# Gate matrix from float32 one-hots, all first products in split halves, block 1's second products on VectorE

## The chip, the cores and the metric

The kernel is one program on one core of a Trainium2 chip. The metric is the device time of one execution in microseconds (us). The engines are called as in the profile: PE is TensorE (PEld its weight loads), DVE is VectorE, ACT is ScalarE, POOL is GpSimd, SP is SyncE, which here issues only DMAs.

## The reference

Two layers work on 512 tokens of width 1024. Each layer is a token mixer (four heads of differential attention and eight of stick-breaking attention) with a LayerNorm, and then PEER, a retrieval over 128 x 128 experts of one neuron each, with a LayerNorm:

```python
q = (xt @ w_query).reshape(T, PEER_HEADS, 2, HALF_Q)
scores = jnp.einsum('thpc,hpnc->thpn', q, sub_keys)
top_s, top_i = lax.top_k(scores, PEER_TOPK)
# ... the 16 best of the sums of both halves, per head: idx, gate = softmax(best_s)
u = expert_u[ic]                                            # 128 experts for each token
act = jax.nn.gelu(jnp.einsum('cd,ced->ce', xc, u), approximate=False)
v = expert_v[ic]
y = jnp.einsum('ce,ced->cd', gc * act, v)
h = layer_norm(DEEPNORM_ALPHA * h + y, ln2_g[l], ln2_b[l])
```

All arrays are float32. Each of the 512 tokens selects 8 x 16 = 128 of the 16384 experts.

## The kernel before

The tokens are four blocks of 128. PEER is computed in two ways that run side by side.

**Blocks 0 and 1 (`BLK_A`) gather.** `indices` selects the experts of a block (`select`, mostly DVE). `gathers` then fetches one row of `expert_u` for each token at a time: POOL issues an indirect DMA of 128 rows of 4 KB, and one DVE instruction (`dot`, "row<-row,ha" in the profile) multiplies it with the tokens and sums. There are 128 such gathers in a block, with six buffers (`gat`). After the GELU the second products follow. For a block in `TOK` (before: both blocks) `token_products` does them on PE: the rows of `expert_v` of one token at a time ("row<-v,idxT") are multiplied by a column of weights in a sliding window (`win`), four matmuls of 32 columns for two tokens. For a block outside `TOK` the function `add` does them on DVE, one gather of `expert_v` rows ("row<-v,idx") and one multiply-add of 128 x 1024 for each of the 128 selections ("ha<-row,c,ha"). The blocks go one after the other: `done["turn ..."]` starts block 1 when block 0 has its products, and layer 1's block 0 when layer 0's block 1 has them. The last instructions of `gathers` are the residual, LayerNorm and, in layer 1, the store of the output.

**Blocks 2 and 3 (`BLK_B`) are dense.** `gates` makes the matrix of gates of all 16384 experts for a block. For four tokens at a time (`NT`) it makes one-hot vectors of the two halves of the expert's number, multiplies one of them by the gate, and PE multiplies the two; the result goes to DRAM (`gdram`, "gd"). Before, the one-hots are bfloat16, and the gate is three bfloat16 pieces, so that a token costs three matmuls; the pieces are spread over ACT, POOL and DVE by `pick`. `dense` goes over 32 chunks of 512 experts: `first` (products with `expert_u` and GELU), `weigh` (the transposed result times the gates, and its halves), `second` (products with `expert_v`, accumulated in four PSUM banks over all chunks). `second` waits for the gates of both blocks. A chunk's weights are 2 MB for `first` and 2 MB for `second`. Except in the first `AHEAD` = 7 chunks of `first`, they are split into two float32r halves by `split`: ACT makes the upper half, and POOL or DVE (by `pick`) subtracts it ("t<-st,t", four parts for each of `first` and `second`); three float32r matmuls take the place of one float32 matmul. The first seven chunks, which run before the gates are ready, use the raw float32 weights on PE ("native").

**What sets the order.** All these are Python generators. `run_threads` holds a planned time for each engine and lets the thread with the smallest ready time less its `lead` go on; `cost(...)` is what a step takes in that plan. An engine named in `soft` doesn't hold the step back. The scheduler behind it fixes one instruction order for each engine, and `bound` keeps instructions within a distance of the plan. So on the chip each engine takes its instructions in a fixed order, and an instruction that waits holds up those behind it. `rest` runs layer after layer: the mixer of blocks 1, 2 and 3, then `dense`. The mixer of layer 1 takes block 1 first, so it starts when block 1 of layer 0 has its LayerNorm; `early` runs the mixer of block 0 ahead. The helper at line 70 (72 in the changed kernel) records every instruction, so all rows have that line.

## Time and profile before

| | us |
|---|---|
| median of three runs | 3627.01 (3624.92 to 3645.93) |
| profiled execution | 3652.87, span 3651.1 |

| engine | busy us | share of the span |
|---|---|---|
| PE | 3081.1 | 84% |
| PEld | 2236.5 | 61% |
| DVE | 2332.3 | 64% |
| POOL | 1802.7 | 49% |
| ACT | 1169.6 | 32% |

The DMA engines move 1035 MB, 284 GB/s over the span. A share over the whole span mixes stages: in layer 0 the mixer and the gates take up to about 1012 us, the dense products up to 1988, and block 1's gathers lie beside them; layer 1 follows in the same order, with its second products from 2870 to 3636. Idle time of an engine costs only where it is the one the others wait for, so the stages are read one by one. A float32 matmul has two records in the profile, a float32r or bfloat16 matmul one.

### The profile page before, as it was taken

The page shows a single profiled execution, that of the slowest core. Times are in us where ns is not written, and L with a number is a line of the kernel's source. Part 1 is how long each engine was busy: PE and PEld are TensorE (multiplying, and loading weights), DVE is VectorE, ACT ScalarE, POOL GpSimd, SP SyncE. Part 2 cuts the span into 40 slices and gives each one's busy share as a digit, 9 for nine tenths or more (in the row PEclk, how much of TensorE's full clock was granted, in tenths as well). Part 3 has the DMA queues.
Part 4 walks back from the last instruction along what each step waited for, and adds up shares of the span by engine and source line. Part 5 has one row for each costly group of instructions (what it writes and reads, how often), then busy time and mean ns, then how long its engine had stood idle before and what let it go on. Part 6 is the DMA issues. An engine that isn't in the chain of part 4 may idle for free.

```text
span 3651.1 us, 45407 instructions
## 1 busy us (share of the span) xinstructions
PE 3081.1 (84%) x16660; PEld 2236.5 (61%) x16660; DVE 2332.3 (64%) x4974; ACT 1169.6 (32%) x1867; POOL 1802.7 (49%) x1368
## 2 busy tenths in 40 slices
PE   7995597888788868899997597888987699999998
PEld 5774473653566756766665486647535577766665
DVE  2588768375668698633336756576757888864335
ACT  2112652120414223333332016613215344343332
POOL 0266426244446375354537752254555666654443
PEclk9997698898889989999999697988997799999999
DMA  5689576577596877689898984566785999989996
GB/s 222 235 331 336 173 268 216 194 262 277 208 364 256 321 279 293 229 329 352 314 347 300 355 321 163 216 235 244 266 305 186 342 345 337 355 295 335 332 355 247
DMA packets 285215, 1035.19 MB, mean 284 GB/s; under 512 B 25408, under 2 KB 91456, under 8 KB 232768
## 3 DMA queue, kind: packets, MB, share of 16 engines
q0 software_dynamic: 147456, 536.94, 40.4%
q1 hardware_dynamic: 137536, 495.36, 36.2%
q8 instruction: 131, 2.15, 0.2%
q14 instruction: 92, 0.75, 0.1%
HBM read 991.30 MB, written 38.80 MB: 282 GB/s over the span
## 4 chain that ended last, share of the span: by engine, by line
PE 33%; issue 9%; POOL 7%; DVE 5%; DMA 4%; ACT 3%; POOLq 0%; another core or an unknown queue 0%; SPq 0%; DVEq 0%; ACTq 0%
PE ps L70 33%; POOL row L70 4%; POOL t L70 3%; DVE d L70 2%; DMA row<-v,idxT 2%; ACT d L70 1%; DVE t L70 1%; ACT L70 1%; DVE row L70 1%; DMA t<-gd 1%; ACT t L70 1%; DMA st<-ut 0%; DMA gd<-st 0%; DVE idf L70 0%; POOL d L70 0%
## 5 line engine op out<-in xcount | busy, mean ns | idle before, releaser
L70 POOL DMA_INDIRECT row<-v,idxT x512 | 566.6, 1107 | 819.0 <-PE ps L70 672.9
L70 PE MATMUL ps<-t,d 128*128 128x512 f32 (+1 forms) x3232 | 808.4, 404 | 147.1 <-POOL t L70 48.9
L70 POOL DMA_INDIRECT row<-u,idx x512 | 672.1, 1313 | 430.1 <-DVE row L70 239.7
L70 PEld LDWEIGHTS ps<-t,d 128*128 128x128 f32 x3232 | 609.6, 196 | 340.3 <-ACT t L70 69.1
L70 DVE SCALAR_TENSOR_TENSOR row<-row,ha 128x1024 f32<-128x1024 f32 x512 | 673.1, 1330 | 164.8 <-DMA row<-u,idx 142.7
L70 DVE TENSOR_TENSOR t<-st,t 128x1024 fp32r<-128x1024 f32 x344 | 472.2, 1412 | 451.6 <-ACT t L70 391.4
L70 PE MATMUL ps<-t,t 128*128 128x512 f32 (+1 forms) x3040 | 664.9, 382 | 15.6 <-DVE t L70 6.9
L70 PEld LDWEIGHTS ps<-t,t 128*128 128x128 f32 (+1 forms) x3040 | 523.1, 197 | 160.3 <-issue 43.3
L70 PE MATMUL ps<-t,st 128*128 128x128 f32 x4096 | 505.8, 284 | 20.9 <-issue 8.9
L70 PEld LDWEIGHTS ps<-t,st 128*128 128x128 f32 x4096 | 491.3, 199 | 42.2 <-issue 27.7
L70 ACT ACTIVATE t<-st 128x1024 fp32r<-128x1024 f32 x456 | 452.8, 1050 | 113.8 <-PE ps L70 88.1
L70 PE MATMUL ps<-st,t 128*128 128x512 f32 x960 | 452.5, 621 | 8.9 <-DMA st<-ut 6.6
L70 POOL TENSOR_TENSOR t<-st,t 128x1024 fp32r<-128x1024 f32 x112 | 284.5, 2551 | 214.0 <-ACT t L70 167.9
L70 ACT ACTIVATE t<-ps 128x512 f32<-128x512 f32 (+1 forms) x192 | 88.8, 492 | 824.8 <-PE ps L70 798.7
L70 PE MATMUL ps<-row,win 128*32 128x512 f32 x2048 | 288.0, 646 | 74.5 <-DMA row<-v,idxT 73.3
L70 PEld LDWEIGHTS ps<-st,t 128*128 128x128 f32 x960 | 183.3, 200 | 247.4 <-issue 241.7
L70 PE MATMUL ps<-d,d 128*128 128x128 bf16 (+1 forms) x1792 | 252.2, 295 | 74.1 <-POOL d L70 30.1
L70 PEld LDWEIGHTS <-d 128*128 128x128 bf16 x1536 | 174.3, 119 | 116.0 <-issue 72.2
L70 ACT COPY st<-ps 128x256 f32<-128x256 f32 x256 | 137.0, 646 | 254.1 <-PE ps L70 216.4
L70 ACT COPY t<-ps 128x512 f32<-128x512 f32 (+4 forms) x180 | 81.1, 459 | 381.0 <-PE ps L70 340.3
L70 DVE TENSOR_TENSOR d<-iota_b,d 128x512 bf16<-128x512 bf16 x246 | 137.5, 598 | 97.5 <-PE ps L70 97.3
L70 POOL TENSOR_TENSOR d<-d,d 128x512 bf16<-128x512 bf16 x132 | 150.8, 1163 | 79.3 <-issue 42.5
(118 smaller groups left out, 2339.6 us busy)
## 6 DMA issues: line engine op xcount, KB each, us to landing
st<-ut SPq DMA_DIRECT2D x128, 1024.0 KB
st<-vd SPq DMA_DIRECT2D x128, 1024.0 KB
st<-w_in SPq DMA_DIRECT2D x48, 1024.0 KB
st<-w_query SPq DMA_DIRECT2D x48, 1024.0 KB
gd<-st SPq DMA_DIRECT2D x32, 1024.0 KB
t<-gd SPq DMA_DIRECT2D x64, 512.0 KB
st<-w_o SPq DMA_DIRECT2D x24, 1024.0 KB
ln<-ln SPq DMA_DIRECT2D x16, 512.0 KB
```

The lines of the kernel that those rows point to most:

```text
L70: r = f(*args, **kwargs)
```

## The change

The one-hots become float32: for each token one `tensor_scalar` makes the one-hot of one half, and one makes the other half's one-hot times the gate, both on DVE; a token then costs one float32 matmul. The plan gives them to DVE alone. `NATIVE = 0` sends the first seven chunks of `first` through `split` as all others. `TOK = [0]` takes block 1 out of `token_products`: its second products go through `add` on DVE. `pace` holds DVE as `soft` for block 0 only, so that block 1's steps wait for DVE's place in the plan. The thread `gates` is spawned with a lead of 40 in place of 6.

```diff
@@ -46,7 +46,9 @@
 HH = PH // 2
 AHEAD = 7
 
-TOK = [0, 1]
+NATIVE = 0
+
+TOK = [0]
 
 REACH = 8
 
@@ -216,8 +218,8 @@
     iota_c = const.tile([P, NCAND, TOPK], BF16, name="iota_c")
     nc.gpsimd.iota(iota_c, pattern=[[1, NCAND], [0, TOPK]], base=0, channel_multiplier=0,
                    allow_small_or_imprecise_dtypes=True)
-    iota_b = const.tile([P, P, NT], BF16, name="iota_b")
-    nc.gpsimd.iota(iota_b, pattern=[[1, P], [0, NT]], base=0, channel_multiplier=0,
+    iota_b = const.tile([P, P], F32, name="iota_b")
+    nc.gpsimd.iota(iota_b, pattern=[[1, P]], base=0, channel_multiplier=0,
                    allow_small_or_imprecise_dtypes=True)
 
 
@@ -563,7 +565,7 @@
                 if n % 2 == 0:
                     SC.setdefault((l, b), []).append(fold(t4(), 8))
                     if n == 0 and b in BLK_B:
-                        spawn(gates(l, b), 6.0)
+                        spawn(gates(l, b), 40.0)
                 ps = psum()
                 for f in range(4):
                     for c in range(DC):
@@ -740,7 +742,7 @@
         c = sel.tile([P, NSEL], F32, name="c")
 
         def pace(dve):
-            return cost(lat=1.2, soft="DVE", DVE=dve, POOL=1.04, DMA=1.6)
+            return cost(lat=1.2, soft="DVE" if b == BLK_A[0] else "", DVE=dve, POOL=1.04, DMA=1.6)
 
         def row(src, s):
             g = gat.tile([P, D], F32, name="row")
@@ -805,7 +807,7 @@
         for half in range(2):
             yield from select(l, b, half, idf, gate)
         idf, gate = (t.rearrange("p h k -> p (h k)") for t in (idf, gate))
-        yield cost(lat=3.0, DVE=2.0, PE=0.7)
+        yield cost(lat=3.0, DVE=1.2, PE=0.7, ACT=0.4)
         ii = a2(I32)[:, :2 * NSEL].rearrange("p (a k) -> p a k", a=2)
         nc.vector.tensor_copy(ii[:, 1, :], idf)
         nc.vector.tensor_single_scalar(ii[:, 0, :], ii[:, 1, :], 7, op=ALU.arith_shift_right)
@@ -815,55 +817,28 @@
         pt = psum()
         for n, src in enumerate((fi[:, 0, :], fi[:, 1, :], gate)):
             nc.tensor.transpose(pt[:, n * P:(n + 1) * P], src, ident)
-        t0, t1 = a2(), a2()
-        gp, ij = fold(t0[:, :3 * P], 3), fold(t0[:, 3 * P:].bitcast(BF16), 2)
-        ijf, gb = fold(t1[:, :2 * P], 2), fold(t1[:, 2 * P:2 * P + 3 * P // 2].bitcast(BF16), 3)
-        nc.vector.tensor_copy(ij.rearrange("p a t -> p (a t)"), pt[:, 0:2 * P])
-        nc.scalar.copy(ijf.rearrange("p a t -> p (a t)"), pt[:, 0:2 * P])
-
-        nc.vector.tensor_copy(gp[:, 0, :], pt[:, 2 * P:3 * P])
-        for k in range(3):
-            nc.vector.tensor_copy(gb[:, k, :], gp[:, k, :])
-            if k < 2:
-                nc.vector.tensor_sub(gp[:, k + 1, :], gp[:, k, :], gb[:, k, :])
-                nc.vector.tensor_copy(gp[:, k, :], gb[:, k, :])
-        shp = [P, P, NT]
-
-        def hots(tg, t0):
-            t = tg * GT + t0
-            hot = a2h().rearrange("p (a j t) -> p a j t", a=2, t=NT)
-            for n in range(2):
-                if pick(ACT=1.7, DVE=0.34) == "ACT":
-                    for k in range(NT):
-                        nc.scalar.activation(hot[:, n, :, k], iota_b[:, :, k], AF.Abs, scale=-1.0,
-                                             bias=ijf[:, n, t + k:t + k + 1])
-                    nc.scalar.activation(hot[:, n], hot[:, n], AF.Relu, scale=-1.0, bias=1.0)
-                else:
-                    nc.vector.tensor_tensor(hot[:, n], iota_b, ij[:, n, t:t + NT].unsqueeze(1).to_broadcast(shp),
-                                            op=ALU.is_equal)
-            w01 = a2h().rearrange("p (a j t) -> p a j t", a=2, t=NT)
-            w2 = a2h()[:, :P * NT].rearrange("p (j t) -> p j t", t=NT)
-            ws = (w01[:, 0], w01[:, 1], w2)
-            for k, w in enumerate(ws):
-                eng = pick(ACT=1.2, POOL=1.0, DVE=0.34)
-                if eng == "ACT":
-                    for n in range(NT):
-                        nc.scalar.activation(w[:, :, n], hot[:, 0, :, n], AF.Copy, scale=gp[:, k, t + n:t + n + 1])
-                else:
-                    (nc.gpsimd if eng == "POOL" else nc.vector).tensor_tensor(
-                        w, hot[:, 0], gb[:, k, t:t + NT].unsqueeze(1).to_broadcast(shp), op=ALU.mult)
-            return hot, ws
+        ijg = fold(a2()[:, :3 * P], 3)
+        nc.scalar.copy(ijg.rearrange("p a t -> p (a t)"), pt[:, :3 * P])
+
+        def hots(t):
+
+
+            hot, w = (fold(a2(), NT) for _ in range(2))
+            for k in range(NT):
+                nc.vector.tensor_scalar(hot[:, k, :], iota_b, ijg[:, 1, t + k:t + k + 1], None, op0=ALU.is_equal)
+                nc.vector.tensor_scalar(w[:, k, :], iota_b, ijg[:, 0, t + k:t + k + 1],
+                                        ijg[:, 2, t + k:t + k + 1], op0=ALU.is_equal, op1=ALU.mult)
+            return hot, w
 
         stg = {}
 
-        def products(tg, t0, hot, ws):
+        def products(tg, t0, hot, w):
             if t0 == 0:
                 stg[tg] = [fold(st_tile().rearrange("p c f -> p (c f)"), 64) for _ in range(2)]
             ps = psum()
             for n in range(NT):
-                for k, w in enumerate(ws):
-                    nc.tensor.matmul(ps[:, n * P:(n + 1) * P], lhsT=hot[:, 1, :, n], rhs=w[:, :, n],
-                                     start=(k == 0), stop=(k == 2))
+                nc.tensor.matmul(ps[:, n * P:(n + 1) * P], lhsT=hot[:, n, :], rhs=w[:, n, :],
+                                 start=True, stop=True)
             ps = fold(ps, NT)
             for a in range(2):
                 nc.scalar.copy(stg[tg][a][:, :, t0:t0 + NT].rearrange("p i t -> p t i"),
@@ -875,8 +850,8 @@
 
         todo = []
         for t in range(0, P, NT):
-            yield cost(lat=0.7, ACT=0.55, PE=0.8)
-            todo.append((t // GT, t % GT, *hots(t // GT, t % GT)))
+            yield cost(lat=1.6, DVE=1.6, ACT=0.9, PE=1.0)
+            todo.append((t // GT, t % GT, *hots(t)))
             if len(todo) > 1:
                 products(*todo.pop(0))
         products(*todo.pop(0))
@@ -901,7 +876,7 @@
 
         def first(ec):
 
-            native = ec < AHEAD
+            native = ec < NATIVE
             for a in range(2):
                 if native:
                     yield cost(PE=6.9, DMA=2.92)
```

The order of the instructions moves with it. Three places of DVE's order follow; names are tiles of the program with their numbers.

**The end of the program.** Names: "t" with "ps" is the residual of a dense block, which needs the last matmul of `second`; "ha" is block 1's result. Before:

```order
L70 TENSOR_TENSOR t_24433<-st,t_24432 128x1024
L70 TENSOR_TENSOR t_24449<-st,t_24448 128x1024
L70 SCALAR_TENSOR_TENSOR ha<-ha 128x1024
L70 BN_STATS aln_st<-ha 128x6 x2
L70 BN_AGGR aln_mv<-aln_st 128x2
L70 TENSOR_SCALAR aln_ve<-aln_mv 128x1
L70 TENSOR_SCALAR ha<-ha,aln_mv,aln_rs 128x1024
L70 TENSOR_TENSOR ha<-ha,row 128x1024 x2
L70 SCALAR_TENSOR_TENSOR t_24478<-t_24478,ps 128x512 x2
L70 SCALAR_TENSOR_TENSOR t_24482<-t_24482,ps 128x512 x2
```

With the change the dense blocks' residual comes earlier in the order, with five more adds between its instructions, and then:

```order
L72 SCALAR_TENSOR_TENSOR ha<-row,c,ha 128x1024
L72 TENSOR_TENSOR t_23764<-t_23764,ln 128x1024
L72 SCALAR_TENSOR_TENSOR ha<-row,c,ha 128x1024 x65
L72 SCALAR_TENSOR_TENSOR ha<-ha 128x1024
L72 BN_STATS aln_st<-ha 128x6 x2
L72 BN_AGGR aln_mv<-aln_st 128x2
L72 TENSOR_SCALAR aln_ve<-aln_mv 128x1
L72 TENSOR_SCALAR ha<-ha,aln_mv,aln_rs 128x1024
L72 TENSOR_TENSOR ha<-ha,row 128x1024 x2
```

Block 1's result stood before the dense residual; now it stands behind it, with 65 adds of 128 x 1024 ahead of it.

**The end of layer 0's dense products**, with the change; "t_12720" is a dense block's residual in its LayerNorm, and "row<-row,ha" are dots of layer 1's block 0:

```order
L72 SCALAR_TENSOR_TENSOR ha<-row,c,ha 128x1024
L72 TENSOR_TENSOR t_12720<-t_12720,ln 128x1024
L72 SCALAR_TENSOR_TENSOR ha<-row,c,ha 128x1024 x57
L72 SCALAR_TENSOR_TENSOR ha<-ha 128x1024
L72 BN_STATS aln_st<-ha 128x6 x2
L72 BN_AGGR aln_mv<-aln_st 128x2
L72 TENSOR_SCALAR aln_ve<-aln_mv 128x1
L72 SCALAR_TENSOR_TENSOR row,c<-row,ha 128x1024
L72 TENSOR_SCALAR ha<-ha,aln_mv,aln_rs 128x1024
```

Before, the same place reads:

```order
L70 TENSOR_TENSOR ha<-ha,row 128x1024 x2
L70 SCALAR_TENSOR_TENSOR t_13164<-t_13164,ps 128x512 x2
L70 SCALAR_TENSOR_TENSOR row,c<-row,ha 128x1024
L70 BN_STATS ln_st<-t_13164 128x6
L70 SCALAR_TENSOR_TENSOR t_13174<-t_13174,ps 128x512
```

Block 1 had its LayerNorm ("ha<-ha,row") ahead of the dense residual; now 57 adds stand between the two.

**A chunk of layer 1's dense products.** "t<-st,t" is a part of `split`, "row<-row,ha" a dot, "t<-ps,t" and "d<-t,d" are `weigh`. Before:

```order
L70 TENSOR_TENSOR t_21287<-st,t_21286 128x1024
L70 TENSOR_TENSOR t_21303<-st,t_21302 128x1024
L70 TENSOR_TENSOR t_21327<-st,t_21326 128x1024
L70 SCALAR_TENSOR_TENSOR row,c<-row,ha 128x1024
L70 TENSOR_TENSOR t_21343<-st,t_21342 128x1024
L70 SCALAR_TENSOR_TENSOR row,c<-row,ha 128x1024 x2
L70 TENSOR_TENSOR t_20993<-ps,t_21183 128x512 x2
L70 SCALAR_TENSOR_TENSOR row,c<-row,ha 128x1024
L70 TENSOR_TENSOR d_21192<-t_20993,d_21191 128x512
```

With the change:

```order
L72 TENSOR_TENSOR t_20405<-st,t_20404 128x1024
L72 TENSOR_TENSOR t_20421<-st,t_20420 128x1024
L72 SCALAR_TENSOR_TENSOR row,c<-row,ha 128x1024 x2
L72 TENSOR_TENSOR t_20442<-st,t_20441 128x1024
L72 TENSOR_TENSOR t_20458<-st,t_20457 128x1024
L72 TENSOR_TENSOR t_20481<-st,t_20480 128x1024
L72 TENSOR_TENSOR t_20497<-st,t_20496 128x1024
L72 TENSOR_TENSOR t_20184<-ps,t_20377 128x512 x2
L72 TENSOR_TENSOR d_20386<-t_20184,d_20385 128x512
```

Between one `weigh` and the next DVE had six splits and seven dots there (POOL had the other two splits); now it has all eight splits, with seven dots or, later, seven adds.

## Rows read from the trace of the kernel before

**Rows 1.** The page: the span, and each engine's busy time (share, count)

```profile
span 3651.1 us, 45407 instructions
PE 3081.1 (84%) x16660; PEld 2236.5 (61%) x16660; DVE 2332.3 (64%) x4974; ACT 1169.6 (32%) x1867; POOL 1802.7 (49%) x1368
```

**Rows 2.** Busy time by stretch: five engines, granted clock, DMA share, GB/s

```profile
875.00:1012.00 137.00, 101.21 (x580) 61.53 (x579) 83.06 (x171) 43.65 (x78) 64.59 (x55) 0.84 0.68 244
1012.00:1407.00 395.00, 321.17 (x1557) 255.43 (x1557) 314.43 (x601) 113.59 (x166) 228.03 (x143) 0.90 0.81 304
1407.00:1988.00 581.00, 551.85 (x2641) 394.47 (x2641) 281.29 (x278) 204.90 (x252) 275.16 (x188) 0.99 0.84 309
1988.00:2045.00 57.00, 3.67 (x20) 3.12 (x20) 45.05 (x75) 2.25 (x4) 40.29 (x32) 0.54 0.92 330
2700.00:2870.00 170.00, 107.79 (x556) 67.39 (x557) 127.04 (x202) 59.50 (x131) 109.15 (x94) 0.76 0.67 242
2870.00:2952.00 82.00, 76.57 (x330) 61.82 (x330) 73.52 (x79) 31.32 (x37) 57.66 (x33) 0.92 0.92 340
2952.00:3217.00 265.00, 252.86 (x1143) 205.62 (x1142) 221.28 (x264) 109.87 (x132) 162.39 (x94) 1.00 0.92 345
3217.00:3636.00 419.00, 411.00 (x2020) 281.05 (x2018) 185.84 (x177) 145.51 (x180) 193.39 (x145) 0.99 0.87 320
```

**Rows 3.** Timeline of PE in layer 1's dense products: start, duration, count

```profile
2964.16 11.05 PE L70 MATMUL ps<-t,t 128*128 128x512 f32 x48
2975.05 1.04 PE L70 MATMUL ps<-ident,t 128*128 128x128 f32 x8
```

**Rows 4.** Timeline of DVE: the gates' multiply in `weigh`, one row a chunk

```profile
2968.57 1.28 DVE L70 TENSOR_TENSOR t<-ps,t 128x512 f32<-128x512 f32 x2
...
3161.68 1.28 DVE L70 TENSOR_TENSOR t<-ps,t 128x512 f32<-128x512 f32 x2
...
3275.67 1.46 DVE L70 TENSOR_TENSOR t<-ps,t 128x512 f32<-128x512 f32 x2
...
3568.74 1.28 DVE L70 TENSOR_TENSOR t<-ps,t 128x512 f32<-128x512 f32 x2
```

**Rows 5.** Timeline: the instruction nearest to a one-hot, with POOL beside it

```profile
1101.83 5.70 DVE L70 TENSOR_SCALAR dg<-ident,rc 128x128 f32<-128x128 f32 x2
1102.68 4.74 POOL L70 TENSOR_TENSOR t<-st,t 128x1024 fp32r<-128x1024 f32 x2
...
2130.64 0.94 POOL L70 DMA_INDIRECT row<-u,idx  x1 [0.31 <-issue]
...
2130.86 0.47 DVE L70 TENSOR_SCALAR dg<-ident,rc 128x128 f32<-128x128 f32 x2
```

**Rows 6.** Groups by form, 875 to 1012: count | busy us, mean ns | idle before

```profile
L70 PE MATMUL ps<-d,d 128*128 128x128 bf16 x384 | 53.8, 295 | 8.9 <-DVE d L70 8.0 <-POOL d L70 0.7
L70 DVE TENSOR_TENSOR d<-d,d 128x512 bf16<-128x512 bf16 x75 | 40.3, 583 | 0.6 <-PE ps L70 0.6
L70 PE MATMUL ps<-st,t 128*128 128x512 f32 x81 | 39.6, 611 | 0.0
L70 DVE TENSOR_TENSOR d<-iota_b,d 128x512 bf16<-128x512 bf16 x64 | 29.3, 497 | 37.3 <-PE ps L70 37.3
```

**Rows 7.** Groups by form, 2952 to 3217: splits and dots (columns as rows 6)

```profile
L70 DVE TENSOR_TENSOR t<-st,t 128x1024 fp32r<-128x1024 f32 x68 | 104.3, 1549 | 44.6 <-ACT t L70 44.6
L70 DVE SCALAR_TENSOR_TENSOR row<-row,ha 128x1024 f32<-128x1024 f32 x76 | 98.4, 1300 | 0.0
L70 ACT ACTIVATE t<-st 128x1024 fp32r<-128x1024 f32 x88 | 87.0, 1057 | 13.5 <-PE ps L70 13.5
```

**Rows 8.** Busy time of instructions on a gathered row, by stretch (columns as rows 2)

```profile
300.00:400.00 100.00, 0.00 (x0) 0.00 (x0) 69.77 (x116) 74.89 (x59) 0.62 0.91 328
```

**Rows 9.** Groups by form, whole span: all instructions of the kind in rows 5

```profile
L70 DVE TENSOR_SCALAR dg<-ident,rc 128x128 f32<-128x128 f32 x64 | 24.7, 406 | 0.0
```

**Rows 10.** Timeline of POOL: a gather issued while DVE works through its dots

```profile
2003.04 1.98 POOL L70 DMA_INDIRECT row<-u,idx  x1 [0.30 <-issue]
```

## Prediction

> **What bounds it now.** I read the page first: PE is busy for 84% of 3651 us, DVE for 64% [rows 1]. That suggests PE, so I read the stretches next. From 1407 to 1988 and from 2870 to 3636 the dense products run; PE is busy for 93% to 98% there, at a granted clock of 0.92 to 1.00 [rows 2]. The timeline gives the price of a chunk on PE: 48 matmuls of `first` take 11.05 us, those of `second` (same shape) as long, two sets of transposes 1.04 each: 24.2 us [rows 3]. The chunks of 2968 to 3161 come every 24.1 us (193.1 us over eight), so there PE alone sets the pace, while block 1's dots run beside it. From 3276 to 3569 they come every 29.3 us (293.1 over ten) [rows 4]: there block 1's second products are on PE too. DVE is far from full in that second half (185.84 of 419 us), but nearly so in the first (221.28 of 265) [rows 2].
>
> Three other stretches are not PE's. From 875 to 1012 and from 2700 to 2870, the wait for block 3's gates, PE is busy for 74% and 63%, at clocks of 0.84 and 0.76 [rows 2]. From 1012 to 1407 the gathers of block 1 meet the early mixer: DVE 80%, DMA 0.81 [rows 2]. From 1988 to 2045, between the layers, PE does 3.67 us of work [rows 2].
>
> **The change, stretch by stretch.**
>
> *Gates.* In the order, 157 of the 336 split matmuls of `first` and block 3's 128 products of one-hots stand behind that block's selection in layer 0. The nearest row to a one-hot is a DVE tensor_scalar of 128 x 128 float32 with a per-partition scalar: two in 0.47 us, so 0.235 each, even with a gather running [rows 5]. Block 3's 256 cost 60 us of DVE, where the bfloat16 form took 40.3 + 29.3 us in the same stretch, and POOL and ACT had more [rows 6]. On PE a float32 product costs as much as a float32 transpose, 0.26 us (four, two records each, in 1.04 [rows 3]): 33 us for 128, against 53.8 [rows 6]. The 157 split matmuls cost 157 x 0.23 = 36 us, where native ones took 39.6 [rows 6]. So PE needs 69 us, DVE 60 plus some ten splits at 1.4 = 74. I take 87 us in place of 137, a gain of 50, and leave the rest for waits. In layer 1, 97 split matmuls remain at that point: 33 + 22 on PE, 60 and some eight splits on DVE. With most of block 1's early dots gone from there I take 105 in place of 170, a gain of 65. The splits that now come earlier (28 for each layer, 1.06 us of ACT each [rows 7]) lie beside block 0's second products and the projections on PE, with ACT busy for 32% [rows 1]; if that cover fails, they cost 30 us a layer.
>
> *1012 to 1407.* The order has 57 dots where 99 stood, and 51 DVE splits where 32 stood: 42 x 1.3 less 19 x 1.5 [rows 7] frees 26 us of DVE, and 42 gathers of 0.52 MB fewer at 304 GB/s [rows 2] free up to 72 us of DMA. I take 40, between the two.
>
> *1407 to 1988.* Nineteen full chunks, three without `first` and 512 records of block 1's products make 2832 PE records; 2641 are there [rows 2], some being lost. Without block 1 on PE, nineteen chunks at 24.4 and three at 13.2 (11.05 and two transposes) give 503 in place of 581. I take 75, since DVE now has all eight splits: 20.1 us a chunk (221.28 over eleven [rows 2]) plus two splits of at most 1.55 [rows 7] is 23.2, 95% of 24.4. What hides the dots and adds is PE's 24.2 us; without that cover the chunk would cost what DVE needs.
>
> *2870 to 3636.* Five chunks as before, 82; 24 at 24.4 and three at 13.2: 707 in place of 766. I take 56.
>
> *The ends.* Here the change gives back. `add` costs no more than a dot, 1.30 [rows 7]. But 128 dots and 128 adds at seven a chunk need 36 chunks, and the dense products end before. Behind layer 0's dense residual stand four adds and then 57, behind layer 1's five and 65. A row alone costs what its gather does: 59 gathers in 100 us with no dense work beside them, 1.7 us each [rows 8]. In layer 0, 55 rows (six are already in buffers) make 94 us, with 15 for the LayerNorms ahead and 8 for block 1's own. Since the mixer of layer 1 takes block 1 first, PE waits for all of it: 117 in place of 57, a loss of 60. Layer 1's dots start that much later against the dense end, but 49 of them stand in a row ahead of the attention before and after, so nothing more is late. At the end, 64 x 1.7 = 109 and 16 more take the place of the 15 us after 3636: a loss of 110.
>
> *Sum.* -50 - 65 - 40 - 75 - 56 + 60 + 110 = -116: 3535 us on the span of 3651 [rows 1]. The median of the runs stands at 3627, 24 below the profiled span, so I scale: 3535 x 3627 / 3651 = 3512. The rest I price at nothing: the shorter iota at the start, and block 1's index transpose and its small SP transfers (16 fall to 8), which go beside the dense chunks; SP's and POOL's queues keep their other DMAs.
>
> **What I cannot read.** A one-hot (two operations, compare and multiply) may cost more than 0.235: the pair beside two POOL subtractions took 5.70 us [rows 5], but in the order POOL keeps 43 subtractions in place of 112. At 0.41, the mean of all such instructions with their collisions [rows 9], block 3's one-hots cost 45 us more in each layer, +90. A lower price gains nothing, as PE then sets the stretch. A row in the tails costs from 1.25 us (0.94 for the issue and 0.31 ahead of it [rows 5]) to 2.28 (1.98 and 0.30, with DVE busy throughout [rows 10]): -54 to +69 over 119 rows. I take 1.7, since it is measured with DVE and POOL both free to pace each other. A chunk costs from 24.2 (PE's work) to 28: that is DVE's 23.2 over the 0.835 busy share it reached in that stretch [rows 2]. Over 43 chunks that is -9 to +155. I take 24.4, because there PE idled for only 5% with DVE at 84%.
>
> The row beside a gather shows the tensor_scalars going through while POOL issues: the gather runs from 2130.64 to 2131.58, the pair from 2130.86 to 2131.33 [rows 5]. The Trainium skill, "SBUF — State Buffer", section "Who interferes with whom", says otherwise: tensor_scalar can enter a two-port mode, and then whichever of VectorE and GpSimd issues first shuts the other out for the whole instruction. By that rule each one-hot could wait for a gather, or a gather for it. The trace agrees for POOL's subtractions (5.70 us) and not for this gather.
>
> **Rivals.**
> 1. *DVE takes PE's place in the dense products* and the kernel ends slower. For: DVE works at 95% of a chunk by my own sum, its order is fixed, and a dot that waits for its row holds the splits behind it, for which PE waits. Against: at 84% PE lost only 5%, and POOL's slow subtractions leave the path. At 28 us a chunk the span is 3535 + 155 = 3690, which is 3666. It decides from 27.9 us a chunk on (3535 + 3.5 x 43 = 3686, or 3662).
> 2. *The gates give nothing.* The order gives PE and ACT the same chunks to do before the gates, and another wait, for scores or w_query, may set 1012 and 2870. For: PE was already at 74% there. Against: DVE alone spent 70 of 137 us on the one-hots there [rows 6], and that work shrinks on every engine. The span is 3535 + 115 = 3650, so 3626: no change.
> 3. *One-hots and gathers shut each other out.* Block 0's 256 gathers of `expert_v` rows run beside block 2's one-hots; if each held DVE for 0.94 [rows 5], that is 241 us of DVE in stretches where it is not full. I put half on the path: 3535 + 120 = 3655, so 3631. The one gather row speaks against it. This is what the Trainium skill's rule above would do here.
> 4. *The tails are cheaper and the early stretch gains more.* At 1.25 us a row (-54) and the DMA's whole 72 us in 1012 to 1407 (-32) the span is 3449, so 3426.
>
> **How the numbers follow.** My forecast has a chance of 0.56, rival 1 0.12, rival 2 0.14, rival 3 0.05, rival 4 0.13. One per cent, about what a measurement of this kernel can tell from no change, is 3591 to 3663. The forecast's own range, 3440 to 3590, is the sum with half of the bounds above. Faster by over 1%: forecast and rival 4, 0.69. Within 1%: rivals 2 and 3, 0.19. Slower: rival 1, 0.12. The range for 8 in 10 leaves out rival 1 and the lower half of rival 4: 3420 to 3635.
>
> **What would show it.** The chunk pace in layer 1 with dots, and again with adds, should be 24 to 25 us, with PE above 95%: above 27 is rival 1. `second` should begin at about 960 in layer 0; at 1012 rival 2 holds. One-hots should stand 0.2 to 0.25 apart; a microsecond between them, with a gather beside, is rival 3. PE should be idle for some 110 us between the layers, and the program should end with 65 adds on DVE and nothing on PE, at 1.7 us a row. If those tails are short, or block 1 ends before the dense products, I have misread the order.

## The result, and the profile after

The changed kernel takes 3586.6 us (median of four runs, 3584.2 to 3601.2), the kernel before, run beside it, 3631.3: a ratio of 0.988, with an interval of 0.986 to 0.991. It is faster by 1.2%, where 3.2% was forecast (3512 us). The time lies within the range, the sign is right, and more than half of the gain is missing.

The page of the changed kernel, to be read against [rows 1]:

```profile
span 3582.5 us, 43439 instructions
PE 2859.1 (80%) x15344; PEld 2225.3 (62%) x15344; DVE 2640.8 (74%) x5853; ACT 1175.9 (33%) x1817; POOL 1519.9 (42%) x1167
```

PE lost 222 us of work and POOL 283, DVE gained 309; the span fell by 69. The first profile of the kernel before was 24 us above its median, though. The first experiment below profiled it again (span 3626.5), and that profile is the fair partner. Busy time by stretch, after; columns as in [rows 2]:

```profile
837.00:1005.00 168.00, 140.04 (x725) 107.82 (x724) 109.85 (x338) 63.06 (x114) 32.88 (x22) 0.89 0.54 210
1005.00:1312.00 307.00, 261.72 (x1254) 209.63 (x1255) 248.32 (x504) 106.08 (x146) 136.00 (x84) 0.94 0.75 268
1312.00:1836.00 524.00, 487.45 (x2128) 392.99 (x2127) 403.73 (x444) 204.19 (x245) 201.88 (x136) 0.96 0.87 320
1836.00:1956.00 120.00, 6.86 (x40) 6.89 (x41) 102.27 (x100) 3.52 (x6) 84.14 (x69) 0.52 0.89 322
1956.00:2623.00 667.00, 544.08 (x3520) 401.59 (x3519) 462.35 (x1523) 212.83 (x400) 317.78 (x275) 0.88 0.79 287
2623.00:2745.00 122.00, 90.32 (x432) 69.11 (x432) 99.01 (x309) 55.92 (x93) 26.04 (x16) 0.88 0.47 177
2745.00:3456.00 711.00, 673.78 (x2976) 543.66 (x2975) 554.87 (x661) 281.35 (x340) 292.49 (x192) 0.98 0.88 321
3456.00:3582.00 126.00, 0.28 (x2) 0.00 (x0) 105.79 (x95) 0.00 (x0) 78.98 (x67) 0.51 0.81 294
```

The same stretches of the kernel before, profiled again (from the first second-product of layer 0 on):

```profile
core 0 of [0], span 3626.5 us
...
1000.00:1392.00 392.00, 319.72 (x1558) 254.28 (x1559) 313.79 (x600) 113.87 (x168) 228.06 (x142) 0.90 0.81 306
1392.00:1976.00 584.00, 555.53 (x2641) 399.00 (x2641) 284.85 (x281) 204.50 (x251) 268.79 (x188) 0.98 0.83 309
1976.00:2033.00 57.00, 3.91 (x22) 3.34 (x22) 45.39 (x76) 2.24 (x4) 37.99 (x32) 0.54 0.91 335
2033.00:2680.00 647.00, 556.85 (x3561) 395.55 (x3561) 428.03 (x1335) 213.34 (x410) 302.08 (x268) 0.90 0.71 260
2680.00:2851.00 171.00, 106.52 (x554) 66.49 (x553) 131.29 (x207) 59.47 (x130) 105.98 (x93) 0.75 0.66 239
2851.00:3611.00 760.00, 734.56 (x3489) 544.92 (x3489) 479.90 (x520) 286.61 (x347) 414.71 (x270) 1.00 0.90 334
3611.00:3626.00 15.00, 0.00 (x0) 0.00 (x0) 10.85 (x18) 0.00 (x0) 1.43 (x2) 0.66 0.26 105
```

The stretch up to the "last selection" ends inside that selection, at the same instruction in both kernels. Put side by side, with what was forecast for each:

| stretch | before | after | change | forecast |
|---|---|---|---|---|
| start to first second-product, layer 0 | 1000 | 1005 | +5 | -50 |
| to chunk 10 | 392 | 307 | -85 | -40 |
| to the end of layer 0's dense products | 584 | 524 | -60 | -75 |
| turn between the layers | 57 | 120 | +63 | +60 |
| layer 1's mixer to the last selection | 647 | 667 | +20 | 0 |
| gates of layer 1 | 171 | 122 | -49 | -65 |
| dense products of layer 1 | 760 | 711 | -49 | -56 |
| end | 15 | 126 | +111 | +110 |
| sum | 3626 | 3582 | -44 | -116 |

Both ends came as forecast. What is missing is 36 us around the selection and the gates of layer 1, 22 in the dense chunks and 10 ahead of chunk 10; 3 and 1 are from the ends.

### The profile page after: what moved, and what is told of

The parts are those of the page before. It is cut to its first block, busy times and chain, and to the rows that moved or that the text cites. A ratio compares the mean times of both kernels' runs of the same rounds, so it can differ in the third digit from the quotient of the medians.

```text
span 3582.5 us, 43439 instructions
## 1 busy us (share of the span) xinstructions
PE 2859.1 (80%) x15344; PEld 2225.3 (62%) x15344; DVE 2640.8 (74%) x5853; ACT 1175.9 (33%) x1817; POOL 1519.9 (42%) x1167
## 4 chain that ended last, share of the span: by engine, by line
issue 26%; PE 13%; POOL 11%; DVE 9%; DMA 7%; ACT 2%; POOLq 0%; SPq 0%; DVEq 0%; ACTq 0%
PE ps L72 13%; POOL row L72 10%; DVE d L72 4%; DVE t L72 2%; DMA row<-u,idx 2%; DVE row L72 2%; DMA row<-v,idxT 1%; DMA d<-keysT 1%; DMA row<-v,idx 1%; ACT d L72 1%; ACT L72 1%; DVE idf L72 1%; DMA t<-gd 1%; POOL t L72 0%; DMA st<-vd 0%
## 5 line engine op out<-in xcount | busy, mean ns | idle before, releaser
L72 PE MATMUL ps<-t,t 128*128 128x512 f32 (+1 forms) x3712 | 848.6, 391 | 81.2 <-DVE t L72 43.6
L72 PEld LDWEIGHTS ps<-t,t 128*128 128x128 f32 (+1 forms) x3712 | 661.1, 200 | 239.4 <-DVE t L72 52.5
L72 POOL DMA_INDIRECT row<-v,idx x256 | 330.1, 1289 | 333.1 <-DVE ha L72 269.4
L72 POOL DMA_INDIRECT row<-v,idxT x256 | 261.4, 1021 | 361.4 <-PE ps L72 269.6
L72 DVE SCALAR_TENSOR_TENSOR ha<-row,c,ha 128x1024 f32<-128x1024 f32 x254 | 325.9, 1283 | 34.3 <-DMA row<-v,idx 27.9
L72 DVE TENSOR_SCALAR d<-iota_b,d 128x128 f32<-128x128 f32 x1024 | 242.2, 318 | 7.5 <-ACT d L72 7.5
L72 POOL TENSOR_TENSOR t<-st,t 128x1024 fp32r<-128x1024 f32 x43 | 109.6, 2560 | 298.6 <-ACT t L72 252.3
L72 PE MATMUL ps<-st,t 128*128 128x512 f32 x512 | 224.7, 594 | 3.1 <-DMA st<-w_o 2.4
L72 PEld LDWEIGHTS ps<-d,d 128*128 128x128 f32 x1280 | 165.7, 195 | 93.9 <-issue 37.6
L72 PE MATMUL ps<-d,d 128*128 128x128 f32 x1280 | 201.8, 298 | 26.6 <-DMA d<-keysT 17.1
```

Of the source, the lines that this page charges most:

```text
L72: r = f(*args, **kwargs)
```

## The experiments

The change has four parts, and the runs take them one by one: **G**, the float32 gates with the lead of 40; **N**, the split first chunks; **T**, block 1's second products on VectorE; **P**, the line of `pace` that makes block 1 wait for DVE's place in the plan. The prediction had no price for P of its own. Diffs are against the kernel before, or the changed one where the text says so. "Mark" is the first second-product of layer 0. Each ratio is against the kernel before, run beside it; beside e5 to e8 that took 3649 us, so for these the ratios say more than the times.

**The kernel before, once more** (no edit).

> The kernel before, unchanged, profiled once more. It prices the last step of the sum, the scaling: I took the profiled span of 3651 us as a true picture, 24 us too long everywhere alike (x 3627/3651). Theory A (that execution was an odd one): the new span lies at the median, 3620 to 3632, and the 20 to 30 us that are missing come out of one or two stretches, so that some of the gaps that I priced as gain were not there in an ordinary execution. Theory B (a profiled execution of this kernel is always that much longer): the span is 3645 to 3660 again and the stretches agree with the first profile within 5 us each.

3633.0 us, span 3626.5: theory A for the time, not for the place, since the 25 us that the first profile was longer are spread: 12 ahead of the mark, 7 between there and layer 1's second products, 6 in those. Measured on this span, the forecast of -116 would have been 3510, so the scaling at the end of the sum did no harm.

**One part alone.** e2 is G, e3 is N:

```diff
+NATIVE = 0
...
-            native = ec < AHEAD
+            native = ec < NATIVE
```

and e4 is T and P:

```diff
-TOK = [0, 1]
+TOK = [0]
...
-            return cost(lat=1.2, soft="DVE", DVE=dve, POOL=1.04, DMA=1.6)
+            return cost(lat=1.2, soft="DVE" if b == BLK_A[0] else "", DVE=dve, POOL=1.04, DMA=1.6)
```

> Only the gates of the change: float32 one-hots on DVE, with the lead of 40; the first seven chunks of first products stay native and block 1's second products stay on PE in both layers. Theory A (the gates' gain was priced rightly in sum, and appears partly behind the first of the second products): 75 to 110 us faster than before, 3520 to 3550 us, with the two stretches that follow the first second-product in layer 0 carrying most of it. Rival (the gates give little; the gain that was measured early in layer 0 came from block 1's dots and from the split first products): 0 to 40 us faster, 3590 to 3627 us.

> Only the split of the first seven chunks of first products; gates in bfloat16 pieces and block 1's products on PE as before. By the price used (a native chunk 13.8 us of PE in the planner's terms, a split one 11.05 measured; DVE and ACT get eight parts a chunk more) PE does 7 x 2.7 = 19 us less in each layer ahead of the gates. Theory A (the wait there ends with DVE's selection and one-hots, so PE's saving is hidden and the 28 parts more of DVE and POOL work delay the gates): 0 to 40 us slower, 3627 to 3667 us. Rival (PE is on the path there): 20 to 40 us faster, 3587 to 3607 us.

> Only block 1's second products on VectorE (and block 1 paced by DVE's plan); gates and first products as before. By the stretches of the two profiles this part takes 57 and 55 us out of the dense products and puts 62 between the layers and 111 at the end. Theory A (this part loses): 3627 + 39 to + 61 = 3666 to 3690 us, with an end of 110 to 130 us after the last matmul of the dense products. Rival (it also carries the early gain of layer 0, 88 us from the first second-product to chunk 10, because fewer dots stand there): 3590 to 3625 us.

All three are slower: G 3702 (ratio 1.020, 1.016 to 1.023), N 3717 (1.024, 1.020 to 1.027), T with P 3659 (1.008, 1.004 to 1.011). For G both theories fall. For N the sign of theory A holds, the size doesn't. T with P loses 27 by the ratio, where 39 to 61 were expected; its mark is at 995, its end is 118 us long. A sum of parts can't make -45 out of +70, +84 and +27.

**Two parts.** e5 is G and N, e6 G with T and P, e7 N with T and P. Against the changed kernel, e5 has `TOK = [0, 1]` and the soft pace, e6 `NATIVE = 7`, e7 the old gates.

> The changed kernel with block 1's second products back on PE in both layers and its pace as before: float32 gates and split first chunks without the third part. Each of the three parts alone was slower than before (+70, +84 and +27 us), all three together 46 faster. Theory A (block 1's part costs what it gives back at the ends, 62 + 111 us against 112 in the dense products, and the other two parts help each other because the float32 gates free ACT and POOL for the splits): 25 to 65 us faster than the changed kernel, 3522 to 3562 us. Theory B (the parts do not add; block 1's part is what lets the other two pay, since it takes PE work away from where the other two put it): slower than the kernel before, 3640 to 3780 us (3780 is the plain sum of the two alone).

> The changed kernel with the first seven chunks of first products native again. Theory A (the split chunks are what uses the time before the gates; without them the float32 gates only bring block 1's dots and layer 1's early mixer ahead of the second products): the loss of the gates alone remains, 3627 + 70 + 27 = 3724, with the first of the second products of layer 0 at 1040 to 1060 us. Theory B (gates and block 1's part suffice, the split costs DVE and ACT what it saves on PE): 3570 to 3600 us, with that mark at 1000 or before.

> The changed kernel with the gates as they were (bfloat16 one-hots in pieces over ACT, POOL and DVE, lead 6). Theory A (the float32 gates carry the gain: the two other parts alone cost 84 and 27): 3680 to 3740 us. Theory B (the gates are worth nothing once the chunks are split and block 1 is on DVE): within 20 us of the changed kernel, 3567 to 3607 us.

e5 takes 3823 (1.046, 1.039 to 1.054): theory B's side, 43 us above its range, and no less than the plain sum of the ratios (1.043). e6 takes 3585 (0.981, 0.973 to 0.989), theory B's time, though its mark is at 1025: at least as fast as the whole change (0.988), without the split chunks. e7 takes 3678 (1.007, 1.003 to 1.010), 2 us below theory A's range. So G loses 2% without T and P and gains 2.7% with them; N costs 2.4% without them and next to nothing with them.

**The early mixer behind the gates.** e8, against the changed kernel:

```diff
-        spawn(early(l, 0), 50.0 if l == 0 else 20.0)
+        spawn(early(l, 0), 50.0 if l == 0 else 0.0)
```

> The changed kernel with the early mixer of layer 1 (block 0's) planned with a lead of 0 in place of 20, and nothing else. In PE's order 128 products of its projections and 16 of 512 columns stand between the last product of one-hots and the first second-product of layer 0 with the change, none before the change; with the lead of 0 the order has 32 and 8 there. Theory A (the gates did come early, at 930 us, and the projections that the plan put in the gap hold the second products until 1005): the mark falls to 940 to 975 us, chunk 10 begins later after it than 307 us, and the whole moves little, since the projections only change places: 3575 to 3600 us. Rival (the mark waits for the gates' way through DRAM or for DVE): it stays at 995 to 1010 us.

The mark falls to 969 and chunk 10 begins 357 us after it: theory A as to the place. It is SP's queue that shows it. First the changed kernel, then e8; "gd<-st" writes gates, "t<-gd" is the read ahead of the mark, "st<-w_in" the early mixer's weights:

```profile
930.03 0.80 SPq L848 DMA_DIRECT2D gd<-st  x2
...
953.40 26.67 SPq L307 DMA_DIRECT2D st<-w_in  x6
980.12 2.52 SPq L912 DMA_DIRECT2D t<-gd  x2
```

```profile
933.75 0.80 SPq L848 DMA_DIRECT2D gd<-st  x2
...
945.58 9.76 SPq L912 DMA_DIRECT2D t<-gd  x2
```

The last gates are written at 931 and 934. The changed kernel issues the read 49 us behind that, after six loads of `w_in`; e8 does it after 11. The whole was expected not to move and took 3627.5 (0.994, 0.990 to 0.997, where the changed kernel has 0.988). Its profile is 31 us longer, with 741 us for layer 1's dense products in place of 711. The order differs there too, so this run doesn't say what the lead alone is worth.

**The pace.** e9 is the changed kernel without P; e10, e11 and e12 have block 1's second products on PE and P: with G and N, with G, and with nothing else.

```diff
-            return cost(lat=1.2, soft="DVE" if b == BLK_A[0] else "", DVE=dve, POOL=1.04, DMA=1.6)
+            return cost(lat=1.2, soft="DVE", DVE=dve, POOL=1.04, DMA=1.6)
```

> The changed kernel with one line as before: block 1's dots and adds no longer wait for DVE's place in the plan (DVE is soft for block 1 again). In the runs of gates alone and of gates with split chunks, 115 and over 100 of block 1's 128 dots stand before the first second-product of layer 0 (18 in the kernel before, 20 in the changed one), and that product starts at 1052 and 1192. Theory P (the pace decides: with the one-hots off POOL, nothing but POOL and DMA holds block 1's gathers back in the plan, and its dots are put among the one-hots and splits): that mark at 1100 to 1200 and 3680 to 3800 us. Theory E (it is the engine of block 1's second products that decides): within 20 us of the changed kernel, 3567 to 3607 us, with the mark at 1000 to 1020.

> The changed kernel with block 1's second products on PE in both layers, but its dots still paced by DVE's plan. With the soft pace this took 3823 us. Theory P (pace): the early stretches stay as with the change (first second-product at 995 to 1015, chunk 10 some 310 to 340 later), the ends give back 62 + 111, and the dense products take 57 + 55 more: 3586 - 61 = 3525, 3500 to 3565 us. Theory E (engine): 3780 to 3830 us again, with the mark near 1190.

> The kernel before with the float32 gates and block 1's pace bound to DVE's plan; the first seven chunks native, block 1's second products on PE. Gates alone with the soft pace took 3702 us. Theory P: gates with block 1's part took 3585; its ends are 62 and 86 us longer than before, its dense products 69 and 45 shorter, so 3585 - 148 + 114 = 3551, 3520 to 3585 us. Theory E: 3690 to 3710 us.

> The kernel before with only block 1's pace bound to DVE's plan. Theory P (the pace matters where something else would let the dots come early; in the kernel before POOL's share of the one-hots holds them back: 18 dots before the first second-product): within 25 us of the kernel before, either way, and the mark at 990 to 1015. Theory E says the same of the mark. If this line alone gains over 40 us, the pace was a gain of its own and not a condition of the other parts.

(The numbers of dots in the first of these were counts of records; a dot leaves two. Ahead of the mark stand 71 dots of block 1 in e2, 128 in e5, 9 in the kernel before and 8 in the changed one.) Without P the whole change takes 3766 (1.036, 1.034 to 1.038), with the mark at 1197: theory P. The stretch ahead of it, all engines, then DVE's groups by form in it:

```profile
845.00:1197.00 352.00, 151.54 (x733) 121.92 (x731) 261.84 (x591) 63.19 (x112) 192.03 (x148) 0.65 0.79 283
```

```profile
L72 DVE SCALAR_TENSOR_TENSOR row<-row,ha 128x1024 f32<-128x1024 f32 x128 | 157.8, 1253 | 41.7 <-DMA row<-u,idx 40.7
L72 DVE TENSOR_SCALAR d<-iota_b,d 128x128 f32<-128x128 f32 x256 | 60.1, 315 | 2.8 <-ACT d L72 2.8
```

All 128 dots stand there: 157.8 us of work and 40.7 of waiting for their rows, and PE is busy for 152 of 352 us at a granted clock of 0.65. In the changed kernel the stretch from 837 to 1005 has 8 dots. P with G takes 3596 (0.990, 0.987 to 0.993), with G and N 3634 (1.000, 0.998 to 1.001), and alone 3698 (1.018, 1.016 to 1.020). So theory P names the condition, but e10 misses its range by 69 us, e11 by 11 and e12 by 39: P costs at the ends. With block 1's products still on PE, the end is 85, 45 and 76 us in these runs in place of 15, since block 1's dots come later; and without P (e9) it is 15 with the adds on DVE.

The ratios to the kernel before, by parts:

| | soft pace | with P | with P and T |
|---|---|---|---|
| nothing else | 1 | 1.018 | 1.008 |
| G | 1.020 | 0.990 | 0.981 |
| N | 1.024 | - | 1.007 |
| G and N | 1.046 | 1.000 | 0.988 |

With P, G gains 1.8% to 2.8%, and T about 1% in each row; N costs up to 1% and never gains. N with P alone was not tried, and no run separates the two halves of G, the float32 one-hots and the lead of 40.

**Where the pace acts.** Against the changed kernel, e13 binds block 1 to DVE's plan only once the layer's gates are made, e14 only until then; e15 (G) and e16 (G and N) are as e14, with the products on PE.

```diff
-            return cost(lat=1.2, soft="DVE" if b == BLK_A[0] else "", DVE=dve, POOL=1.04, DMA=1.6)
+            return cost(lat=1.2, soft="DVE" if b == BLK_A[0] or f"gates {l} {BLK_B[-1]}" in done else "", DVE=dve, POOL=1.04, DMA=1.6)
```

(e14; e13 has `not in`.)

> The changed kernel with block 1's pace bound to DVE's plan only once the gates of the layer are made, and soft until then. Theory Q (what the pace line is worth is decided ahead of the gates: there it keeps block 1's dots out of DVE's order): as with the soft pace throughout, first second-product at 1150 to 1210, 3700 to 3790 us. Theory R (it is decided in the dense products, where the pace sets seven dots or adds a chunk): the mark at 1000 to 1020, within 40 us of the changed kernel.

> The changed kernel with block 1's pace bound to DVE's plan until the gates of the layer are made, and soft from then on. Theory Q: the mark stays at 1000 to 1020; the dots end earlier (the order has all 128 of layer 0 within sixteen chunks in place of twenty), 57 adds in place of 77 stand behind the dense products of layer 1 and 23 in place of 68 behind those of layer 0; at 1.7 us a row the ends are 34 and 76 us shorter, and what of it the dense products take back is open: 3500 to 3580 us. Theory R: 3680 us or more.

> The kernel before with the float32 gates alone, and block 1's pace bound to DVE's plan until the gates of the layer are made; first seven chunks native, block 1's second products on PE. Theory Q: the gates' gain without the early dots and without the ends: the parts of the run with the strict pace up to the dense products of layer 1 (2774 us), and the dense products and the end of the kernel before (760 + 15): 3549, 3520 to 3580 us. Theory R: near the run of gates alone, 3690 to 3710 us.

> As the run before it, with the first seven chunks split as well. Theory Q: in the factorial runs the split cost 0 to 40 us beside the float32 gates once the pace was strict, so 3520 to 3620 us. Theory R: 3780 to 3830 us.

e13: mark at 1200, 3663 us (1.008, 1.005 to 1.011), with 128 dots ahead of the mark: theory Q's mark, 37 us below its range. e14: mark at 1026, 3589 (0.989, 0.986 to 0.993), 9 above Q's range and far from R's 3680. So bound ahead of the gates alone, P is worth all that it is worth in the changed kernel: theory Q. e14's shorter end, 95 us in place of 126, doesn't show in its time. But the dense products are not without weight: e13 and e9, without any P, have the same mark (1200 and 1197) and the same end (15 us), and from the mark to the end of layer 0's dense products e13 takes 821 us where e9 takes 904. Bound only behind the gates, P still takes off 103 of the 180 us that e9 loses. As the 128 dots stand ahead of the mark in both, it is the adds that are bound there. e15 takes 3605 (0.993, 0.991 to 0.996) and e16 3625 (0.998, 0.996 to 1.000): nothing of R, but 25 and 5 above Q's ranges. e15's end is 44 us, not 15, and its dense products of layer 0 take 603 us after chunk 10, not 584.

**What paces the rows at the ends.** Against the changed kernel, e17 halves the adds, e18 the fetches:

```diff
-                    nc.vector.scalar_tensor_tensor(y, g, c[:, s:s + 1], y, op0=ALU.mult, op1=ALU.add)
+                    nc.vector.scalar_tensor_tensor(y[:, :512], g[:, :512], c[:, s:s + 1], y[:, :512], op0=ALU.mult, op1=ALU.add)
```

```diff
-                todo.append((s, row(vr[l], s)))
+                todo.append((s, todo[-1][1] if s % 2 else row(vr[l], s)))
```

> The changed kernel with block 1's adds on 512 of the 1024 columns (it leaves out half of block 1's second products in both layers); every row is still fetched whole, and the order is the same up to a few instructions. It asks what paces the rows of the two ends and of the last chunks. Theory G (the fetch paces them: 1.7 us a row at the ends, with the DMA engines 81% to 89% busy there): the end after the dense products stays at 115 to 130 us, the turn at 110 to 120, the time within 25 us of the changed kernel, 3560 to 3590. Theory V (VectorE's 1.29 us for an add paces them): 65 and 57 rows cost 0.65 less each, and the chunks with adds get shorter: 3480 to 3520 us.

> The changed kernel with only every second row of block 1's second products fetched; each fetched row is added twice with both weights (it leaves out the other 64 rows of expert_v in each layer), so DVE does all 128 adds. Theory G: at the ends a row then costs DVE's 1.29 in place of 1.7: 65 and 57 rows, 27 and 23 us less, and some 5 to 15 us in the chunks with adds: 3510 to 3540 us. Theory V: within 15 us of the changed kernel, 3570 to 3600.

e17: 3563 us (0.981, 0.977 to 0.984), 24 below the changed kernel, so G's number; e18: 3589 (0.989, 0.985 to 0.992), so V's number. The two answers exclude each other, and the rows show why. Instructions on a row at the end of layer 1, in the changed kernel, in e17 and in e18:

```profile
3490.00:3570.00 80.00, 0.00 (x0) 0.00 (x0) 67.41 (x53) 57.71 (x50) 0.50 0.96 352
```

```profile
3480.00:3559.00 79.00, 0.00 (x0) 0.00 (x0) 43.85 (x59) 54.87 (x55) 0.50 1.01 397
```

```profile
3492.00:3574.00 82.00, 0.00 (x0) 0.00 (x0) 79.78 (x63) 48.77 (x27) 0.50 0.64 192
```

53 adds in 80 us, 1.51 each; 59 in 79, 1.34; 63 in 82, 1.30. (Over the whole end it is 1.63, 1.42 and 1.42.) Neither alone paces the changed kernel's row: with half the adds the fetches set 1.34, with half the fetches the adds set 1.30, and together they hold each other up. The last section shows one way in which they do. e18 loses its gain before, in the chunks with dots (741 us of dense products in place of 711), which it leaves as they were but for small shifts of the order. So what takes back the gain of all the variants at 3580 to 3600 is not settled.

## Why the prediction was right in part

The steps that failed are these. That "nothing more is late" once the turn is paid for stood at 0 and measured +20. The gates of layer 1 were taken at 105 us and measured 122. 24.4 us was taken for every chunk, and a chunk measured 28.2 and 25.8 with dots and 23.0 with adds. The 128 products of layer 1's early mixer that now stand ahead of layer 0's second products were not looked for. And the line of `pace` had no price, though without it the change loses.

**The ends** were right. 61 and 69 adds start behind the dense products (4 and 57, 5 and 65 by the order), at 1.65 and 1.63 us a row where 1.7 was taken (110.8 us for 68 steps at the end of layer 1): +63 and +111 where +60 and +110 stood. PE is idle for 113 of the 120 us of the turn, as said. But the reason given was half of it: the ends are long because P puts block 1's rows late. P without T has an end of 76 us (e12), T without P, beside G and N, one of 15 (e9).

**The one-hots** were right. A row of block 2's, with gathers beside them on POOL:

```profile
563.00 17.30 DVE L72 TENSOR_SCALAR d<-iota_b,d 128x128 f32<-128x128 f32 x76 [1.56 <-ACT d L72]
...
567.50 1.00 POOL L72 DMA_INDIRECT row<-v,idxT  x1 [6.17 <-PE ps L72]
...
568.80 1.05 POOL L72 DMA_INDIRECT row<-v,idxT  x1 [0.30 <-issue]
```

76 in 17.3 us is 0.228 each, where 0.235 was taken, and the gathers take their 1.0 us beside them. Rival 3, built on the Trainium skill ("SBUF — State Buffer", section "Who interferes with whom"), didn't come: the trace doesn't agree that such a tensor_scalar and a gather shut each other out.

**Gates of layer 0, and 1012 to 1407**: together -80 where -90 stood, but -50 and -40 became +5 and -85. The step that failed is "157 of the 336 split matmuls of `first` and block 3's 128 products of one-hots stand behind that block's selection", taken as all that does. In the order, 128 products of the early mixer's projections now stand there as well, and SP has its weights ahead of the gates' read; none did before. They were not looked for. The last gates were written at 931, early enough for the forecast 960: e8, which writes its last at 934, has its mark at 969. From the selection's last reduction to the mark it is 139 us in both profiles of before, 151 in the changed kernel and 110 in e8, with most of these products behind the mark: so even then the gain is 29, not 50. What the early mixer does there comes off again before chunk 10 (307 us, where e8 has 357). That -50 and -40 miss by only 10 together is such an exchange, and confirms neither.

**Gates of layer 1**: -49 where -65 stood, in 122 us where 105 were priced. The way of the gates through DRAM was left to "waits":

```profile
2713.84 0.33 DVE L72 TENSOR_SCALAR d<-iota_b,d 128x128 f32<-128x128 f32 x1
...
2715.37 0.80 SPq L848 DMA_DIRECT2D gd<-st  x2
...
2728.68 1.29 SPq L912 DMA_DIRECT2D t<-gd  x2
...
2743.24 1.29 DVE L72 TENSOR_TENSOR t<-ps,t 128x512 f32<-128x512 f32 x2 [3.45 <-DMA t<-gd]
```

From the last one-hot to the first multiply with gates it takes 29 us; 13 of them pass between the write's issue on SP and the read's. Another 27 went by from the mark inside the last selection (2623) to block 3's first one-hot (2650), and the selection's last reduction begins only at 2641. The 64 us of one-hots between are the 60 of the sum.

**"Nothing more is late"** is the step that cost most, 20 us. The first dot of layer 1's block 0 and the mixer's first projections on PE, before (second profile) and after:

```profile
1956.52 1.21 DVE L70 SCALAR_TENSOR_TENSOR row<-row,ha 128x1024 f32<-128x1024 f32 x1
...
2033.85 22.41 PE L70 MATMUL ps<-t,st 128*128 128x128 f32 x192
```

```profile
1941.89 1.22 DVE L72 SCALAR_TENSOR_TENSOR row<-row,ha 128x1024 f32<-128x1024 f32 x1
...
1954.29 21.62 PE L72 MATMUL ps<-t,st 128*128 128x128 f32 x192
```

The dots began 77 us ahead of the mixer before, and 12 after: 35 of them were done by then, and 7. From there the last selection (the same mark) is 646 us away before and 669 after. In the sixteen profiles of this case in which no dot of block 1 stands in that stretch, it falls by 1.1 us for each dot done ahead (a straight line, correlation -0.79), and a dot takes 1.2. But two runs with 31 dots ahead have 608 (e11) and 665 (e3). No run moves these dots alone, so the cause is argued, not shown.

**The dense chunks**: -60 and -49 where -75 and -56 stood. The term that was mis-sized is the 24.4 us a chunk. 24.2 us was misread as PE's work: a chunk has one set of transposes, so PE needs 23.1 (2 x 11.05 + 1.04), and the 24.1 of before held a wait of 1 us for POOL's split, as this row of PE in its second profile:

```profile
2958.12 8.47 PE L70 MATMUL ps<-t,d 128*128 128x512 f32 x36 [0.99 <-POOL t L70]
```

The count of records had said so. The prediction reckoned 2832 for 1407 to 1988 and took the 191 that are missing for lost. None is: 1056 of `second`, 912 of `first`, 512 of block 1's products, 160 of transposes and one more make the 2641, and 160 are twenty sets of eight, one a chunk:

```profile
L70 PE MATMUL ps<-ident,t 128*128 128x128 f32 x160 | 23.7, 277 | 0.0
```

After, a chunk takes 23.0 us with adds (3284 to 3422, six chunks; 1594 to 1802 in layer 0, nine, 23.1). With dots it takes 28.2 in layer 0 (1312 to 1594, ten chunks) and 25.8 in layer 1 (2817 to 3229, sixteen), and the one chunk between dots and adds 32. The ten and the nine of layer 0, then four with dots and six with adds of layer 1:

```profile
1312.00:1594.00 282.00, 247.53 (x1041) 196.91 (x1041) 195.70 (x248) 101.31 (x123) 109.04 (x69) 0.93 0.81 288
1594.00:1802.00 208.00, 206.04 (x938) 168.71 (x937) 177.27 (x167) 89.63 (x108) 79.08 (x58) 1.00 0.93 353
```

```profile
2817.00:2924.00 107.00, 96.73 (x418) 76.65 (x416) 78.66 (x104) 38.98 (x48) 44.23 (x28) 0.97 0.85 303
...
3284.00:3422.00 138.00, 137.54 (x626) 112.46 (x624) 121.55 (x114) 58.92 (x73) 51.77 (x42) 1.00 0.97 365
```

PE and DVE in the ten, then in the four:

```profile
L72 PE MATMUL ps<-t,d 128*128 128x512 f32 x481 | 131.4, 430 | 35.0 <-DVE t L72 30.6 <-ACT t L72 4.4
```

```profile
L72 DVE SCALAR_TENSOR_TENSOR row<-row,ha 128x1024 f32<-128x1024 f32 x65 | 80.2, 1254 | 77.9 <-DMA row<-u,idx 77.9
```

```profile
L72 PE MATMUL ps<-t,d 128*128 128x512 f32 x192 | 50.3, 416 | 9.8 <-DVE t L72 7.9 <-ACT t L72 1.7
```

```profile
L72 DVE SCALAR_TENSOR_TENSOR row<-row,ha 128x1024 f32<-128x1024 f32 x28 | 33.6, 1220 | 11.9 <-DMA row<-u,idx 11.9
```

PE waits for DVE's splits, and DVE, busy for only 196 of 282 us and 79 of 107, waits for the rows of its dots. That is what rival 1 named, a dot that waits for its row and holds up the splits behind it, and in layer 0's chunks with dots at rival 1's price of 28. It doesn't make the whole slower, because the chunks with adds, 16 of the 43, run at PE's 23.0, below the 24.4 of the sum. That the mean of the nineteen and of the twenty-four (25.8 and 25.2) is still near 24.4 comes from two errors of opposite sign, which is luck. The row's arrival decides it, not DVE's load: with adds DVE is busy for 88% (121.55 of 138) and PE waits for nothing. Why the rows come later in layer 0 than in layer 1 is open.

**The sum itself.** The terms were worked out for the change as a whole, and as such they are 72 us off. But they were given as if G, N and T each carried theirs. The runs show that G gains only with P, which had no price: without that line the same change is 3.6% slower, with all of block 1's dots ahead of the mark. The reason is read from the plan: the one-hots no longer lie on POOL, and with DVE soft nothing else kept block 1's gathers back. As no run has the float32 one-hots with the old lead, it is argued. N's split matmuls were part of the gates' terms; the runs show no gain of its own for N.

## What to carry to other kernels

Where a planner sets the order, a resource that a change frees is given to the next thread in line: look in the new order for what was moved into the gap, on every engine and on the DMA queue, before a gap is priced as gained. Take a change's small scheduling lines as parts of their own; here one condition in a cost call decided between 1.2% faster and 3.6% slower. And when a stage is shortened, ask what begins its work by the end of another stage: a chain of gathers that starts relative to one mark and is needed relative to another can be late by the difference.

## What the runs showed of the hardware

A gather's issue on POOL that starts during a DVE instruction with two inputs from SBUF lasts to the end of that instruction and some 0.8 us more. Two rows of the changed kernel, where four adds follow each other at 1.31 us each, and two of e18, where twelve do at 1.32:

```profile
3488.00 5.25 DVE L72 SCALAR_TENSOR_TENSOR ha<-row,c,ha 128x1024 f32<-128x1024 f32 x4
3489.09 1.02 POOL L72 DMA_INDIRECT row<-v,idx  x1 [0.30 <-issue]
```

```profile
3504.37 15.81 DVE L72 SCALAR_TENSOR_TENSOR ha<-row,c,ha 128x1024 f32<-128x1024 f32 x12
3504.61 1.87 POOL L72 DMA_INDIRECT row<-v,idx  x1 [0.77 <-DVE ha L72]
```

The first issue starts 1.09 us into an add, so 0.22 are left of it; it takes 1.02. The other starts 0.24 us into one, 1.08 are left, and it takes 1.87. In the changed kernel all 184 issues that start during an add fit this within 0.06 us (the rest of the add plus 0.81, median; at least 0.94), and an issue that starts with DVE idle takes 0.94. The add that follows doesn't hold the issue again, and the adds keep their 1.3 us. So the adds draw out the fetches: in the two stretches of rows shown for e17 and the changed kernel an issue takes 1.00 and 1.18 us on the mean. The Trainium skill, "SBUF — State Buffer", section "Who interferes with whom", says that a VectorE instruction with two SBUF inputs contends with a GpSimd instruction that reads SBUF. The trace agrees with it, if what waits is the reading of the row numbers in `idx`; which part of the issue waits, no run shows. One-hots, 0.23 us long and with a single tensor input, leave the issue at 1.00 to 1.05 us (rows above). With half the adds the gathers at the end alone moved 397 GB/s, with the DMA engines full (1.01).
